# Turning three more q/k groups by GpSimd block copies, and issuing sixteen copies in two halves

## The chip, the core and the metric

The kernel runs on one core of one Trainium2 chip. Its time is the device time of one execution in microseconds (us), as the median of several runs. Five engines of the core matter: TensorE (PE in the profile; its weight loads are listed apart as PEld), VectorE (DVE), ScalarE (ACT), GpSimd (POOL) and SyncE (SP), which here only issues DMAs.

## What is computed

Two layers of a bidirectional encoder over 256 tokens of 2048 features, in float32. Each layer has a parallel mixer and a gated feed-forward part; the change lies in the mixer of the second layer. Cut to what matters here:

```python
for l in range(DEPTH):                                    # 2 layers
    h = rmsnorm(x, norm_mix[l]) * (1.0 + sc_a) + sh_a
    qa, ka, va, qb, kb, vb, ga, gb = split_cols(h @ w_in[l])
    qa = rotary_partial(rmsnorm(qa.reshape(B, S, HA, 128), qn_a[l]), pos)   # HA = 8 heads
    ka = rotary_partial(rmsnorm(ka.reshape(B, S, GA, 128), kn_a[l]), pos)   # GA = 2 heads
    ya = window_attention(qa, ka, va, sink_a[l]) @ w_proj_a[l]
    qb = rmsnorm(qb.reshape(B, S, HB, 128), qn_b[l])                        # HB = 8 heads
    kb = rmsnorm(kb.reshape(B, S, HB, 128), kn_b[l])
    yb = neighbourhood_attention(qb, kb, vb, rel_bias_b[l]) @ w_proj_b[l]
    merged = jax.nn.sigmoid(ga) * ya + jax.nn.sigmoid(gb) * yb
    x = x + gt_a * (merged @ w_out[l])
    ...
```

For the scores of a head, q and k are needed with the head's 128 features on the partitions. The projection gives them with tokens on the partitions, since the norm and the rotary tables work on rows. So each q/k block of 128 tokens by 128 features has to be transposed. The softmax probabilities p have to be transposed as well.

## The kernel before

**Weights and units.** All weights stream in as blocks of 128x128, sixteen to a *unit* of 1 MB. For each half unit ACT writes a rounded copy (L326, tile `hl`) and DVE writes the remainder (L327), so that TensorE can multiply in three passes: with the high part of the weight twice and with the low part once. The pool of `hl` has four buffers of half a unit. A unit is followed by a *tick* (`Stream.tick`), in which the background work of the pacer `bg` runs: functions that were deferred, then a share of the attention job.

**Groups.** The 4608 columns of q, k and v go in nine groups, numbered 0 to 8, of 512 columns and 64 blocks, that is four units and four ticks each (`tokens`, L406 to L408, 512 columns at a time). In the order of the code: 0 is k and v of the first mixer, 1 and 2 are its q; 3 is k, 4 is v and 5 is q of the first four heads of the second mixer; 6, 7 and 8 are the same of its last four. Before group 0 come eight units of a gate, after group 8 the rest of that gate.

**A q/k group** goes through `qk_rows`: ACT squares and sums (L578), DVE scales the sums (L471), GpSimd takes the inverse root (`qrs`, L472). Three ticks later DVE multiplies rows and roots into the tile `qn` (the norm, L588), of which there is one buffer. Another tick later `turn` transposes, in one of two ways:

- Not moved: eight transposes on TensorE (L624) into PSUM tiles `qtp`, which share the three buffers of the pool `ax` with the attention's scores, sums and outputs; ACT reads them out with the gain (L625).
- Moved (groups 0, 1, 2 and 8 of the second layer): DVE transposes within 32x32 blocks (L612), sixteen GpSimd copies put the blocks in place (`moved_blocks`, L298), and three ticks later (`QK_STEPS`) ACT scales them in place (L616), held in program order. The norm of a moved group is held in program order on DVE too.

**Attention.** In the second layer all sixteen heads transpose p the moved way: DVE (L304), sixteen GpSimd copies (`turned_blocks`), and one step of the attention job later ACT splits the result into `pT` (L418), held in program order. The job takes 0.4 steps a tick in the second layer, starts behind group 1, and takes in one new head a step.

**Order.** A planner orders each engine's instructions by their place in the program and by when it takes them to be ready; what is "held in program order" is not moved against its engine's other instructions. What a tick issues is thus a place in the order, and not a time.

Of the kernel before, what the change touches and what calls it, by code (L numbers as in the profile page):

```python
# [15 lines left out]
P = 128  # L16
# [5 lines left out]
HA, GA, HB = 8, 2, 8  # L22
# [8 lines left out]
BLOCK = 32  # L31
# [53 lines left out]
SCORES_3 = (1,)  # L85
EARLY = {1: 2}

MOVED_QK = [(), (0,1,2,8)]
QK_STEPS = 3
MOVED = [(0,0), (8,8)]  # L90
STEPS = [1, 1]
# [50 lines left out]
def encoder(ctx: ExitStack, tc: tile.TileContext, a: dict, out: bass.AP):  # L142
    nc = tc.nc
# [143 lines left out]
    def later(n, fn):  # L287

        if n == 0:
            fn()  # L290
        else:
            bg.defer(lambda: later(n - 1, fn))

    def moved_blocks(dst, src):

        for b in range(0, P, BLOCK):
            for a in range(0, P, BLOCK):
                nc.gpsimd.tensor_copy(  # L298
                    out=dst[a : a + BLOCK, :, :, b : b + BLOCK], in_=src[b : b + BLOCK, :, :, a : a + BLOCK]
                )  # L300

    def turned_blocks(src, rows, n):

        nc.vector.transpose(out=rows, in_=src)  # L304
        blocks = rows.rearrange("p t (n k) -> p n t k", n=n)
        dst = src.rearrange("p t (n k) -> p (t n k)", n=n).rearrange("p (n t k) -> p n t k", n=n, t=2)
        moved_blocks(dst, blocks)

    def unit_steps(l, u, by_halves=False):

# [256 lines left out]
            nc.vector.tensor_tensor(out=z[:], in0=ps[:, :S], in1=self.rbs[:], op=ALU.mult)  # L567
            return z, sh

    def qk_rows(pss, heads, rot, gain, dst, then, moved=False):  # L570

        cols = 0
        n = heads * HEAD
# [10 lines left out]
        def norm():  # L584
            qn = at.tile([P, 8 * HEAD], F32, name="qn", tag="qn", bufs=1)[:, : 2 * n]
            qn = qn.rearrange("p (t h d) -> p t h d", t=2, d=HEAD)
            for t, ps in enumerate(pss):
                product = nc.vector.tensor_tensor(  # L588
                    out=qn[:, t],
                    in0=ps[:, cols : cols + n].rearrange("p (h d) -> p h d", d=HEAD),  # L590
                    in1=rs[:, t * heads : (t + 1) * heads].unsqueeze(2).broadcast_to([P, heads, HEAD]),
                    op=ALU.mult,
                )
                if moved:
                    tc.keep_in_program_order(product)
            if rot is not None:
                x1, x2 = qn[:, :, :, :HALF], qn[:, :, :, HALF:ROT]
                tab = [rot[:, i].unsqueeze(2).broadcast_to([P, 2, heads, HALF]) for i in range(4)]
                tm = []
                for i in range(2):  # L600
                    z = ev.tile([P, S], F32, name=f"rt{i}", tag="z")
                    z = z[:].rearrange("p (i t h d) -> p i t h d", i=2, t=2, h=4)
                    tm += [z[:, 0, :, :heads], z[:, 1, :, :heads]]
                for i, src in enumerate((x1, x2, x2, x1)):
                    nc.vector.tensor_tensor(out=tm[i], in0=src, in1=tab[i], op=ALU.mult)
                nc.vector.tensor_tensor(out=x1, in0=tm[0], in1=tm[1], op=ALU.subtract)
                nc.vector.tensor_tensor(out=x2, in0=tm[2], in1=tm[3], op=ALU.add)
            bg.defer(lambda: turn(qn))

        def turn(qn):  # L610
            if moved:
                nc.vector.transpose(out=qn, in_=qn)  # L612
                moved_blocks(dst.rearrange("p h (t s) -> p h t s", t=2), qn.rearrange("p t h d -> p h t d"))

                def scaled():
                    tc.keep_in_program_order(nc.scalar.activation(out=dst, in_=dst, func=AF.Identity, scale=gain))  # L616
                    then()

                later(QK_STEPS, scaled)
                return  # L620
            for t in range(2):
                ps = ax.tile([P, 4, P], F32, name="qtp", tag="ax")
                for h in range(heads):
                    nc.tensor.transpose(ps[:, h], qn[:, t, h], ident[:])  # L624
                nc.scalar.activation(  # L625
                    out=dst[:, :, t * P : (t + 1) * P], in_=ps[:, :heads], func=AF.Identity, scale=gain
                )
            then()
# [17 lines left out]
    def attend(q, k, v, p, mask, scale, sink, o, rows=None):  # L646
# [161 lines left out]
    for l in range(L):  # L808
# [117 lines left out]
        for pi, (groups, gates) in enumerate(parts):  # L926
            last = pi == len(parts) - 1
            for g, part in enumerate(groups):
# [21 lines left out]
                    for t in range(2):  # L950
                        nc.scalar.copy(rows[:, t, vcol:], pss[t][:, vcol:])
                if g == 0:
                    qk_rows(pss, GA, rots[1], gains[:, 1:2], kTa, turned, g in MOVED_QK[l])
                elif g < 3:
                    qk_rows(pss, 4, rots[0], gains[:, 0:1], dst, turned, g in MOVED_QK[l])
# [248 lines left out]
```

## Time and profile before

| | us |
|---|---|
| median of 3 runs | 2656.88 |
| lowest and highest run | 2656.29, 2665.97 |
| profiled execution | 2655.52 |
| its span in the profile | 2653.7 |
| GpSimd busy in the whole span | 229.5 |
| of it copies of p (L298, 256 of them) | 147.5 |
| of it copies of q and k (L298, 64 of them) | 45.6 |

The profile is one execution. A row of the timeline has the start, the time taken, engine, line, operation, tile written and tiles read, shape and count, and in brackets the idle time of the engine before it and what ended that. A row of the waits has the waiting engine and line, what it waited for, the sum, how often and the longest. "Line" is the line of the kernel as printed above. TensorE's matmuls overlap: one is listed with its full duration, while the next starts before it ends, so what a matmul costs is read from starts.

### The profile page before, as it was taken

The page shows a single profiled execution, that of the slowest core. Times are in us where ns is not written, and L with a number is a line of the kernel's source. Part 1 is how long each engine was busy: PE and PEld are TensorE (multiplying, and loading weights), DVE is VectorE, ACT ScalarE, POOL GpSimd, SP SyncE. Part 2 cuts the span into 40 slices and gives each one's busy share as a digit, 9 for nine tenths or more (in the row PEclk, how much of TensorE's full clock was granted, in tenths as well). Part 3 has the DMA queues.
Part 4 walks back from the last instruction along what each step waited for, and adds up shares of the span by engine and source line. Part 5 has one row for each costly group of instructions (what it writes and reads, how often), then busy time and mean ns, then how long its engine had stood idle before and what let it go on. Part 6 is the DMA issues. An engine that isn't in the chain of part 4 may idle for free.

```text
span 2653.7 us, 51014 instructions
## 1 busy us (share of the span) xinstructions
PE 2640.4 (99%) x21164; PEld 2554.8 (96%) x21164; DVE 2122.8 (80%) x2979; ACT 1412.8 (53%) x2280; POOL 229.5 (9%) x345
## 2 busy tenths in 40 slices
PE   9999999999999999999999999999999999999999
PEld 7888899999999999999998889999999999999999
DVE  8898998997987888788976778868888866655664
ACT  5445865456653555355554666655565445544553
POOL 0001100000000000000002558620000000000000
PEclk9999999999999999999999999999999999999999
DMA  9987779885877778787856666667757765555554
GB/s 368 350 329 294 266 294 348 330 309 209 291 288 297 294 285 297 287 293 281 303 206 254 252 235 223 255 255 265 278 185 287 296 246 192 192 199 194 194 191 143
DMA packets 102042, 700.42 MB, mean 264 GB/s; under 512 B 12721, under 2 KB 15025, under 8 KB 17969
## 3 DMA queue, kind: packets, MB, share of 16 engines
q1 hardware_dynamic: 101810, 697.17, 71.5%
q8 instruction: 165, 2.70, 0.4%
q14 instruction: 67, 0.55, 0.1%
HBM read 695.03 MB, written 2.10 MB: 263 GB/s over the span
## 4 chain that ended last, share of the span: by engine, by line
PE 88%; DVE 6%; DMA 2%; issue 1%; ACT 1%; POOL 1%; SPq 0%; DVEq 0%; POOLq 0%; ACTq 0%
PE ps L343 25%; PE ps L345 25%; PE ps L344 25%; PE ps_t L407 4%; PE ps_t L408 4%; PE ps_t L406 4%; DVE hl L327 2%; DVE aw L233 2%; DMA aw<-in_aw 1%; PE sc L651 1%; PE po L689 1%; DMA w<-in_ws 1%; ACT hl L326 1%; POOL p L298 0%; POOL qrs L472 0%
## 5 line engine op out<-in xcount | busy, mean ns | idle before, releaser
L327 DVE TENSOR_TENSOR hl<-w,hl 128x1024 fp32r<-128x1024 f32 x928 | 1131.4, 1226 | 318.2 <-ACT hl L326 314.2
L326 ACT CAST hl<-w 128x1024 fp32r<-128x1024 f32 x928 | 970.3, 1049 | 744.0 <-PE ps L345 495.7
L343 PE MATMUL ps<-h,hl 128*128 128x256 f32 x3328 | 923.9, 278 | 1.3 <-DVE ya L970 0.6
L344 PE MATMUL ps<-h,hl 128*128 128x256 f32 x3328 | 921.1, 277 | 0.0
L345 PE MATMUL ps<-h,hl 128*128 128x256 f32 x3328 | 921.0, 277 | 0.0
L343 PEld LDWEIGHTS ps<-h,hl 128*128 128x128 f32 x3328 | 624.9, 188 | 2.3 <-DVE ya L970 0.8
L344 PEld LDWEIGHTS ps<-h,hl 128*128 128x128 f32 x3328 | 625.4, 188 | 0.4 <-DVE h L501 0.2
L345 PEld LDWEIGHTS ps<-h,hl 128*128 128x128 f32 x3328 | 624.4, 188 | 0.0
L233 DVE CUSTOM_DVE_ANT_0 aw<-aw,cact,ab 128x2048 f32<-128x2048 f32 x189 | 444.1, 2350 | 47.7 <-DMA aw<-in_aw 46.6
L407 PE MATMUL ps_t<-hl,h 128*128 128x512 f32 x576 | 225.3, 392 | 0.6
L406 PE MATMUL ps_t<-hl,h 128*128 128x512 f32 x576 | 223.3, 393 | 2.4 <-ACT h L500 1.6
L408 PE MATMUL ps_t<-hl,h 128*128 128x512 f32 x576 | 224.6, 391 | 0.0
L1049 DVE SCALAR_TENSOR_TENSOR u<-ps,cw,u 128x255 f32<-128x255 f32 x304 | 146.3, 481 | 71.9 <-ACT u L1047 67.9
L1047 ACT ACTIVATE u<-ps,cw 128x256 f32<-128x256 f32 x152 | 85.7, 564 | 192.3 <-PE ps L345 192.2
L345 PE MATMUL ps<-merged,hl 128*128 128x256 f32 x512 | 142.1, 278 | 0.5 <-DVE hl L327 0.4
L344 PE MATMUL ps<-merged,hl 128*128 128x256 f32 x512 | 141.7, 277 | 0.0
L343 PE MATMUL ps<-merged,hl 128*128 128x256 f32 x512 | 141.7, 277 | 0.0
L344 PE MATMUL ps<-act_o,hl 128*128 128x256 f32 x512 | 141.7, 277 | 0.0
L345 PE MATMUL ps<-act_o,hl 128*128 128x256 f32 x512 | 141.6, 277 | 0.0
L343 PE MATMUL ps<-act_o,hl 128*128 128x256 f32 x512 | 141.4, 277 | 0.0
L406 PEld LDWEIGHTS ps_t<-hl,h 128*128 128x128 f32 x576 | 108.0, 188 | 25.9 <-ACT h L500 2.7
L407 PEld LDWEIGHTS ps_t<-hl,h 128*128 128x128 f32 x576 | 108.2, 188 | 24.5 <-DVE hl L327 2.7
(244 smaller groups left out, 4805.6 us busy)
## 6 DMA issues: line engine op xcount, KB each, us to landing
w<-in_ws SPq DMA_DIRECT2D x463, 1024.0 KB, 4.9
aw<-in_aw SPq DMA_DIRECT2D x189, 1024.0 KB, 6.2
p<-in_bias SPq DMA_DIRECT2D x16, 256.0 KB, 4.4
x<-in_xT SPq DMA_DIRECT2D x4, 512.0 KB, 5.1
aw_o<-in_aw SPq DMA_DIRECT2D x2, 1024.0 KB, 12.6
out<-x SPq DMA_DIRECT2D x16, 128.0 KB, 3.3
w<-in_ws SPq DMA_DIRECT2D x2, 512.0 KB, 11.7
aw_b<-in_aw SPq DMA_DIRECT2D x1, 1024.0 KB, 18.3
```

Of the source, the lines that this page charges most:

```text
L233: nc.vector.tensor_tensor_reduce(out=raw[:], in0=raw[:], in1=cact[:], scale=1.0, scalar=ab[:, i : i + 1], op0=ALU.mult, op1=ALU.add, accum ...
L326: nc.scalar.copy(hl[:, 0], r)
L327: nc.vector.tensor_tensor(out=hl[:, 1], in0=r, in1=hl[:, 0].bitcast(F32), op=ALU.subtract)
L343: nc.tensor.matmul(out, hi, act[0], start=first, stop=False)
L344: nc.tensor.matmul(ps[:, :S], hi, act[1], start=False, stop=False)
L345: nc.tensor.matmul(out, lo, act[0], start=False, stop=last)
L406: nc.tensor.matmul(ps[:], xh, hi, start=kc == kcs[0], stop=False)
L407: nc.tensor.matmul(ps[:], xh, lo, start=False, stop=False)
L408: nc.tensor.matmul(ps[:], xl, hi, start=False, stop=kc == kcs[-1])
L651: nc.tensor.matmul(sc[:, t], q[i][:, t * P : (t + 1) * P], k[j], start=i + j == 0, stop=(i, j) == by(q)[-1])
L1047: nc.scalar.activation(out=u, in_=ps, func=AF.Identity, scale=w[:, 1:2], bias=w[:, 3:4])
L1049: nc.vector.scalar_tensor_tensor(out=u[:, to], in0=ps[:, of], scalar=w[:, j : j + 1], in1=u[:, to], op0=ALU.mult, op1=ALU.add)
```

## The change

Three things change:

- Groups 3, 5 and 6 of the second layer are moved too, so that all its q/k groups are. Their gain (L616) is issued five ticks behind the turn instead of three (`gain_late`).
- `moved_blocks` issues eight of its sixteen copies at once and defers the other eight by one tick. For a head's p the second eight are issued at the latest ahead of the split into `pT` (`rest()`). This holds for all moved groups and for all sixteen heads of the second layer.
- Which norms are held in program order is now a parameter of its own (`pinned`), true for all groups of the second layer. They are also all the moved ones, so groups 3, 5 and 6 gain the hold.

```diff
-MOVED_QK = [(), (0,1,2,8)]
+MOVED_QK = [(), (0,1,2,3,5,6,8)]
...
+    def once(fn):
+
+        due = [fn]
+
+        def run():
+            if due:
+                due.pop()()
+
+        return run
+
     def moved_blocks(dst, src):
 
-        for b in range(0, P, BLOCK):
-            for a in range(0, P, BLOCK):
-                nc.gpsimd.tensor_copy(
-                    out=dst[a : a + BLOCK, :, :, b : b + BLOCK], in_=src[b : b + BLOCK, :, :, a : a + BLOCK]
-                )
+        def half(first):
+            for b in range(first, first + P // 2, BLOCK):
+                for a in range(0, P, BLOCK):
+                    nc.gpsimd.tensor_copy(
+                        out=dst[a : a + BLOCK, :, :, b : b + BLOCK], in_=src[b : b + BLOCK, :, :, a : a + BLOCK]
+                    )
+
+        half(0)
+        rest = once(lambda: half(P // 2))
+        later(1, rest)
+        return rest
...
-        moved_blocks(dst, blocks)
+        return moved_blocks(dst, blocks)
...
-    def qk_rows(pss, heads, rot, gain, dst, then, moved=False):
+    def qk_rows(pss, heads, rot, gain, dst, then, moved=False, pinned=False, gain_late=False):
...
-                if moved:
+                if pinned:
                     tc.keep_in_program_order(product)
...
-                later(QK_STEPS, scaled)
+                later(QK_STEPS + (2 if gain_late else 0), scaled)
...
-            turned_blocks(p[:], rows(), 2)
+            rest = turned_blocks(p[:], rows(), 2)
             for _ in range(STEPS[sink is None]):
                 yield
+            rest()
...
-                    qk_rows(pss, 4, None, gains[:, 3:4] if g in (3, 6) else gains[:, 2:3], dst, turned, g in MOVED_QK[l])
+                    qk_rows(pss, 4, None, gains[:, 3:4] if g in (3, 6) else gains[:, 2:3], dst, turned, g in MOVED_QK[l], l == 1, g in (3, 5, 6))
```

The two other calls of `qk_rows`, for groups 0 to 2, get the same two arguments.

More of the change, by code (lines that the diff above doesn't have):

```diff
@@ L952, in encoder @@
                 if g == 0:
-                    qk_rows(pss, GA, rots[1], gains[:, 1:2], kTa, turned, g in MOVED_QK[l])
+                    qk_rows(pss, GA, rots[1], gains[:, 1:2], kTa, turned, g in MOVED_QK[l], l == 1, g in (3, 5, 6))
                 elif g < 3:
-                    qk_rows(pss, 4, rots[0], gains[:, 0:1], dst, turned, g in MOVED_QK[l])
+                    qk_rows(pss, 4, rots[0], gains[:, 0:1], dst, turned, g in MOVED_QK[l], l == 1, g in (3, 5, 6))
                 elif vcol is None:
-                    qk_rows(pss, 4, None, gains[:, 3:4] if g in (3, 6) else gains[:, 2:3], dst, turned, g in MOVED_QK[l])
+                    qk_rows(pss, 4, None, gains[:, 3:4] if g in (3, 6) else gains[:, 2:3], dst, turned, g in MOVED_QK[l], l == 1, g in (3, 5, 6))
                 else:
```

## The prediction

> **What bounds the kernel now.** I read the page first (busy shares and the chain of waits).
>
> ```profile
> PE 2640.4 (99%) x21164; PEld 2554.8 (96%) x21164; DVE 2122.8 (80%) x2979; ACT 1412.8 (53%) x2280; POOL 229.5 (9%) x345
> ```
>
> ```profile
> POOL 0001100000000000000002558620000000000000
> ```
>
> ```profile
> PE 88%; DVE 6%; DMA 2%; issue 1%; ACT 1%; POOL 1%; SPq 0%; DVEq 0%; POOLq 0%; ACTq 0%
> ```
>
> TensorE is busy for 99% of the span and carries 88% of the chain: work taken from it is time, as long as the others keep feeding it. GpSimd is nearly idle as a whole, but the second part, in 40 slices, shows where it works: one slice of 66 us at 80%. That is the stretch that the change loads further, so averages say nothing here and I looked at the stretch alone, by windows (columns: stretch, length, busy time of PE, PEld, DVE, ACT and POOL, clock, DMA).
>
> ```profile
> 1486.00:1595.00 109.00, 107.79 (x517) 90.03 (x516) 80.93 (x133) 70.74 (x147) 53.60 (x103) 1.00 0.62 231
> 1595.00:1618.00 23.00, 23.00 (x164) 21.48 (x163) 18.14 (x27) 15.33 (x40) 17.33 (x26) 1.00 0.58 212
> ```
>
> These 132 us hold groups 4 to 8 of the second layer, the turning of groups 3, 5 and 6, and the first attention heads. TensorE idles for 109.00 - 107.79 = 1.2 us in all of them. DVE has 132 - 99 = 33 us free, ACT 46, GpSimd 61; the clock is 1.00. So there are two things to ask: what the removed TensorE work is worth, and whether the added DVE and GpSimd work makes something late that TensorE waits for.
>
> **What is removed.** First the transposes of groups 3, 5 and 6 (tile view of the transposes' result, 1400 to 1700 us), then how the first eight stand in TensorE's timeline, then the second eight and what followed them.
>
> ```profile
> L624 PE MATMUL qtp<-ident,qn x24: 270/273/273, 1504.9 to 1580.5; 128*128 128x128 f32 x24
> L625 ACT ACTIVATE packB<-qtp,gains x6: 669/690/694, 1505.6 to 1581.3; 128x512 f32<-128x512 f32 x6
> ```
>
> ```profile
> 1504.71 0.39 PE L408 MATMUL ps_t<-hl,h 128*128 128x512 f32 x1
> 1504.94 1.03 PE L624 MATMUL qtp<-ident,qn 128*128 128x128 f32 x8
> 1505.73 0.48 PE L406 MATMUL ps_t<-hl,h 128*128 128x512 f32 x1
> 1506.05 0.39 PE L407 MATMUL ps_t<-hl,h 128*128 128x512 f32 x1
> ```
>
> ```profile
> 1552.38 1.03 PE L624 MATMUL qtp<-ident,qn 128*128 128x128 f32 x8
> 1553.16 0.95 PE L689 MATMUL po<-pT,vA 128*128 128x256 f32 x6
> 1553.95 0.39 PE L406 MATMUL ps_t<-hl,h 128*128 128x512 f32 x1
> 1555.41 0.95 PE L651 MATMUL sc<-kA,qA 128*128 128x256 f32 x6 [1.06 <-ACT packB L625]
> ```
>
> Matmuls overlap, so a duration is not what one costs; starts are. The transposes start 0.23 us behind the matmul before them (1504.71, 1504.94), as one such matmul does behind another. Without the eight, L406 would start at 1504.94 and L407 at 1505.17; it starts at 1506.05. Eight transposes cost 0.88 us, and three times that is **-2.6 us**.
>
> The last fence shows a second cost. After L406 at 1553.95 the scores should start at 1554.18 and start at 1555.41, 1.2 us late, put down to ACT's L625: the scores need a PSUM buffer of the three that they share with the transposes' results, and ACT must first read those out. Without transposes there is nothing to read out: **-1.2 us**, the whole idle time of that window. A bound on the other side is 0, if the scores then wait for some other buffer; I take the row.
>
> ACT loses six L625 and gains three L616 of twice the size.
>
> ```profile
> L616 ACT ACTIVATE packB<-packB,gains x1: 1154/1154/1154, 1636.8 to 1636.8; 128x1024 f32<-128x1024 f32 x1
> ```
>
> ```profile
> L612 DVE STREAM_TRANSPOSE qn<-qn x4: 706/1239/1246, 1430.8 to 1617.1; 128x1024 f32<-128x1024 f32 x3, 128x512 f32<-128x512 f32 x1
> ```
>
> That is 6 x 0.69 - 3 x 1.15 = 0.7 us less, under its 46 us of free time: 0. DVE gains three L612 of 1.24 us, 3.7 us against 33 free: 0 by themselves, 3.7 if each fell where TensorE waits for DVE.
>
> **What is added on GpSimd.** 48 copies of 32x256. The GpSimd timeline around them:
>
> ```profile
> 1451.96 14.58 POOL L298 COPY packA<-qn 32x256 f32<-32x256 f32 x16 [5.72 <-DVE qn L612]
> ...
> 1501.54 9.90 POOL L298 COPY p<-spare 32x128 f32<-32x128 f32 x16 [12.49 <-DVE spare L304]
> ...
> 1532.29 6.30 POOL L298 COPY p<-packA 32x128 f32<-32x128 f32 x16 [7.02 <-DVE packA L304]
> 1538.67 1.63 POOL L472 TENSOR_TENSOR qrs<-qss,mhalf 128x8 f32<-128x8 f32 x1
> 1553.04 7.64 POOL L298 COPY p<-packA 32x128 f32<-32x128 f32 x16 [12.73 <-DVE packA L304]
> 1560.76 1.63 POOL L472 TENSOR_TENSOR qrs<-qss,mhalf 128x8 f32<-128x8 f32 x1
> 1569.27 10.38 POOL L298 COPY p<-packA 32x128 f32<-32x128 f32 x16 [6.87 <-DVE packA L304]
> 1583.15 9.75 POOL L298 COPY p<-packA 32x128 f32<-32x128 f32 x16 [3.51 <-DVE packA L304]
> 1595.02 11.84 POOL L298 COPY p<-packA 32x128 f32<-32x128 f32 x16 [2.11 <-DVE packA L304]
> 1609.18 1.64 POOL L472 TENSOR_TENSOR qrs<-qss,mhalf 128x8 f32<-128x8 f32 x1 [2.32 <-DVE qss L471]
> 1613.15 10.62 POOL L298 COPY p<-packA 32x128 f32<-32x128 f32 x16 [2.33 <-DVE packA L304]
> 1623.83 11.64 POOL L298 COPY packB<-qn 32x256 f32<-32x256 f32 x16
> ```
>
> Sixteen such copies took 14.58 us (group 1) and 11.64 us (group 8). Three times that is 35 to 44 us, against 61 free: it fits as a sum, at 82 to 88% of the engine. So the question is order. Three engines wait for these copies: ACT (L418 casts p, L616 scales; both are held in program order, so its weight casts L326 stand behind), and DVE (the norm L588 cannot overwrite qn before the copies have read it, and it waits for qrs, which queues behind copies; its weight subtractions L327 stand behind).
>
> Group 3: GpSimd's work before head 0, the qrs of this group, ends at 1501.54 - 12.49 = 1489.05. A norm (1.29 for its two halves, in a row below) and a transpose later it is some 1492; GpSimd is idle until 1501.54. Its copies fill 1492 to 1504 or 1507, and head 0's end 2 to 5 us later than now. Group 5: behind the qrs that ends at 1538.67 + 1.63 = 1540.3 come norm, weight work and transpose, so its copies fall between some 1545 and 1560, in the 12.73 us in which GpSimd idles now, and partly into head 3's. Group 6: its norm ends at 1562.43 + 1.29 = 1563.7 (row below), so they are ready from about 1565, ahead of head 4's, which move by 11.6 to 14.6 us and push heads 5 and 6.
>
> The eight-and-eight matters here. At 1532.29 the sixteen copies of a head run ahead of a qrs, and the norm waited for it. The waits of 1486 to 1618 and the second such case:
>
> ```profile
> DVE qn L588 <- POOL qrs L472: 11.6, 3, 5.7
> ...
> PEld ps_t L407 <- DVE hl L327: 0.6, 1, 0.6
> ```
>
> ```profile
> 1559.32 0.17 DVE L471 TENSOR_SCALAR qss<-qss 128x8 f32<-128x8 f32 x1 [0.44 <-ACT qsq L578]
> ...
> 1562.43 1.29 DVE L588 TENSOR_TENSOR qn<-ps_t,qrs 128x512 f32<-128x512 f32 x2 [2.94 <-POOL qrs L472]
> ```
>
> This calibrates what lateness costs: DVE stood still for 11.6 us in three waits, and TensorE waited once for DVE's L327, 0.6 us in its weight loader, because weights are split some 5 us ahead (four half-unit buffers of 2.7 us each, two of them in use). The point where that lead was used up is the one behind the norm at 1562.43; there, every further microsecond is a microsecond of TensorE. With halves the qrs can go ahead of the last eight copies: up to 1.3 us earlier (its sums were ready at 1559.32 + 0.17 = 1559.5, and it began at 1560.76), and that wait goes: -0.6. Or head 3's first eight, behind group 5's sixteen, push it: 1545 + 14.6 + 3.8 = 1563.4 instead of 1560.76, +2.7. Between -0.6 and +2.7 I take +0.8, nearer the gain, as GpSimd is idle for 12.73 us before head 3. That is the one new cost on the path.
>
> ACT's held casts of p, by ACT's timeline, for the two heads most exposed:
>
> ```profile
> 1512.78 0.62 ACT L418 CAST pT<-p 128x512 fp32r<-128x512 f32 x1
> ...
> 1587.50 0.62 ACT L418 CAST pT<-p 128x512 fp32r<-128x512 f32 x1
> ```
>
> Head 0's copies end at 1511.44 now, 1.3 us before its cast; 2 to 5 later makes ACT wait 0.7 to 3.7. Head 4's end at 1579.65, 7.9 us before; 11.6 to 14.6 later makes ACT wait 3.7 to 6.7. ACT has 46 of 132 us free and casts weights some 5 us ahead of their use: I take 0, with up to 3.7 + 6.7 = 10.4 us if none of it is hidden.
>
> Splitting the heads' own copies (16 heads) moves eight copies back in the order by one weight unit, 24 matmuls x 0.23 = 5.5 us of TensorE. It adds no copy; where GpSimd is backlogged it changes nothing. 0.
>
> **Sum:** -2.6 - 1.2 + 0.8 = -3.0 us. The profiled execution took 2655.52 (span 2653.7 and 1.8 around it), so 2652.5; it lies 1.4 below the median of the runs, and from that it is 2653.9. I forecast 2653.7.
>
> **The rivals.** *Slower: GpSimd's queue runs late (20%).* The place is 1569 to 1624: 10.38 + 9.75 + 11.84 + 1.64 + 10.62 = 44 us of work in 54.5; group 6 makes it 56 to 59, so the queue overflows into group 8's copies, and the casts held for heads 0 and 4 wait up to 10.4 us. For it: the overflow is arithmetic. Against: the 11.6 us of DVE waits that cost 0.6. It decides once a held wait exceeds the lead of some 5 us. Two thirds of 10.4 unhidden is +7, less 3: +4, 2661. If the casts of heads 5, 6 and 7 came as late as head 4's, 3 x 6.7 = 20 us more, it would pass +13.
>
> *Nothing comes of it (13%).* The saved 3.8 us return as waits for weight halves, through the 3.7 us of L612: 2656.9. Against: of the stretch's 1.2 us of idle TensorE the read-out of the transposes has 1.06, L327 next to nothing.
>
> *Copies and DVE block each other (5%).* These rows stand for it and against it:
>
> ```profile
> L298 POOL COPY packA<-qn x48: 279/395/2365, 1431.7 to 1486.9; 32x256 f32<-32x256 f32 x32, 32x128 f32<-32x128 f32 x16
> ```
>
> ```profile
> L327 DVE TENSOR_TENSOR hl<-w,hl x38: 1180/1224/1310, 1490.3 to 1599.7; 128x1024 fp32r<-128x1024 f32 x38
> ```
>
> A copy takes 0.395 us at the median and up to 2.365: it waits for something as long as a DVE instruction. DVE's subtraction hardly stretches (1.224, at most 1.310). If each of 16 copies of group 5 held DVE for a whole 0.4 us just where the lead is used up, that is 6.4 us, less 3: +3.4, 2660. The Trainium skill (SBUF — State Buffer, section "SBUF: two separate sides") says that GpSimd and a DVE operation with two SBUF inputs take one shared port pair as an exclusive lock for a whole instruction, and the other blocks. By that rule both sides pay; the trace agrees for the copies' side, and shows 0.09 us at most on DVE's durations.
>
> **How the numbers follow.** The forecast has 62%; its own range is 2651.3 to 2656.6 (-0.6 and +2.7 in place of +0.8, and a microsecond for the spread of the runs). The range is 2650.5 to 2661.0: down to everything gained, counted from the profiled execution (2655.5 - 2.6 - 1.2 - 0.6 = 2651.1, and a little), up to the queue's rival. 0.5% of this kernel is 13 us, about what a measurement can tell from no change. All of TensorE's work and idle time at stake is 4.4 us, so faster by 13 is 2%, for a gain I don't see. Slower by 13 is the queue's rival at its worst: 8%. The rest, 90%, is no difference.
>
> **What would show it.** Right: no L624 in the second layer; TensorE's idle time in 1486 to 1595 under 1.5 us; the end of group 8 some 3 us earlier, counted from the start of group 3; GpSimd at 80% or more there; the qrs at 1538 and 1560 no later than now. Wrong: TensorE waiting for DVE's L327 or ACT's L326 by several us; ACT's L418 or L616 listed as waiting for GpSimd's L298 for over 5 us; DVE's L588 waiting for copies; DVE's L327 stretched.

## The result, and the profile after

| | before | after |
|---|---|---|
| median of 15 runs each, us | 2656.55 | 2667.56 |
| lowest and highest | 2654.03, 2667.57 | 2663.27, 2671.49 |
| profiled execution | 2655.52 | 2667.3 |
| its span | 2653.7 | 2665.5 |

The ratio of the times is 1.0028 with a 95% interval of 1.0019 to 1.0037: slower by some 7.4 us (5.0 to 9.8). The medians differ by more, 11.0 us; four of the fifteen runs of before took 2663 to 2668. As a time the result lies outside the forecast's range; as a change it lies within the 0.5% that were called no difference.

The first part of the page of after, and its chain:

```profile
PE 2644.7 (99%) x21140; PEld 2557.4 (96%) x21140; DVE 2126.6 (80%) x2982; ACT 1406.9 (53%) x2277; POOL 274.3 (10%) x393
...
PE 85%; DVE 7%; POOL 4%; issue 2%; ACT 2%; DMA 1%; SPq 0%; DVEq 0%; POOLq 0%; ACTq 0%
```

The 24 transposes are gone (21164 matmuls became 21140), yet TensorE is busy for longer. GpSimd took 44.8 us more and went from 1% to 4% of the chain. To place the loss, two distances serve for every kernel below. The *stretch* is from the first to the last start of the groups' first weight pass (L406 before, L422 after). The *path* runs from that first start to the first matmul that reads oB, the second mixer's projection; it also holds what follows group 8. The rows of before, by source line, and those of after:

```profile
L406 PE MATMUL ps_t<-hl,h x288: 387/390/476, 1395.1 to 1603.2; 128*128 128x512 f32 x144
L343 PE MATMUL ps<-oB,hl x128: 275/277/283, 1793.4 to 1836.9; 128*128 128x256 f32 x128
```

```profile
L422 PE MATMUL ps_t<-hl,h x288: 387/389/632, 1398.3 to 1614.0; 128*128 128x512 f32 x144
L359 PE MATMUL ps<-oB,hl x128: 275/276/283, 1805.2 to 1848.7; 128*128 128x256 f32 x128
```

The stretch grew from 208.1 to 215.7 us (+7.6), the path from 398.3 to 406.9 (+8.6). The remaining 3.2 us between the two profiled executions lie ahead of group 0, where the change touches nothing; the interval of the ratio holds 8.6. So 7.6 of the 8.6 us are lost by the last start of group 8. Both distances are read from one profiled execution of each kernel. Kernels that run the same instructions in the same order (after and e1, before and e18 below) agree in them within 0.4 us, while group 0 starts anywhere from 1393.5 to 1400.1 us in the kernels' profiles; so the distances are the finer measure. The windows of after (columns as before):

```profile
1486.00:1595.00 109.00, 102.66 (x472) 84.88 (x472) 79.55 (x122) 66.10 (x144) 84.95 (x128) 0.98 0.58 209
1595.00:1618.00 23.00, 20.79 (x96) 17.23 (x95) 13.06 (x20) 12.93 (x28) 20.55 (x41) 0.93 0.58 224
1581.50:1585.00 3.50, 3.50 (x10) 2.76 (x11) 3.50 (x5) 0.00 (x0) 3.33 (x5) 0.57 0.46 108
1612.50:1615.50 3.00, 3.00 (x10) 2.38 (x9) 1.34 (x2) 0.73 (x4) 2.75 (x7) 0.54 0.99 341
```

TensorE idles for 6.3 + 2.2 = 8.5 us where it idled for 1.2, and in two short windows the granted clock is 0.57 and 0.54. GpSimd works for 84.95 + 20.55 = 105.5 of the 132 us, that is 80%, just under the forecast's 82 to 88%. Yet the sum is not what matters; its timeline is:

```profile
1501.85 13.74 POOL L309 COPY packB<-qn 32x256 f32<-32x256 f32 x16 [8.57 <-DVE den L682]
1515.64 6.46 POOL L309 COPY p<-spare 32x128 f32<-32x128 f32 x16
1526.81 12.21 POOL L309 COPY p<-packA 32x128 f32<-32x128 f32 x16 [4.72 <-DVE packA L320]
1539.82 7.12 POOL L309 COPY p<-packA 32x128 f32<-32x128 f32 x16 [0.81 <-DVE packA L320]
1547.02 1.64 POOL L488 TENSOR_TENSOR qrs<-qss,mhalf 128x8 f32<-128x8 f32 x1
1551.32 16.16 POOL L309 COPY packB<-qn 32x256 f32<-32x256 f32 x16 [2.66 <-DVE qn L628]
1567.52 9.00 POOL L309 COPY p<-packA 32x128 f32<-32x128 f32 x16
1576.60 1.64 POOL L488 TENSOR_TENSOR qrs<-qss,mhalf 128x8 f32<-128x8 f32 x1
1580.31 10.29 POOL L309 COPY p<-packA 32x128 f32<-32x128 f32 x16 [2.07 <-DVE packA L320]
1590.66 13.60 POOL L309 COPY packB<-qn 32x256 f32<-32x256 f32 x16
1604.32 5.21 POOL L309 COPY p<-packA 32x128 f32<-32x128 f32 x16
```

Times of before and after are compared from the start of group 0, so 3.2 us are taken off those of after. Group 3's copies start at 1501.85 (1498.7 in the time of before, not 1492), after 8.57 us in which GpSimd idled, and head 0's come behind them. (They wait for the transpose L628, which ends at 1501.7 in DVE's rows below; the row names a short DVE instruction behind it.) From there to 1609.5 GpSimd stands for only 10.3 of 107.7 us. The halves never part (sixteen in a row each time), and group 5's root stands behind sixteen copies of a head: it ends at 1548.7, 1545.5 in the time of before, that is 5.2 us later than before (1540.3). Group 5's copies run where head 3's stood. What waits for this, from the waits of 1486 to 1618:

```profile
DVE qn L604 <- POOL qrs L488: 10.4, 2, 5.9
...
PE ps_t L423 <- DVE hl L343: 8.5, 4, 3.0
...
DVE packA L320 <- POOL p L309: 8.3, 2, 7.1
ACT pT L434 <- POOL p L309: 6.9, 1, 6.9
```

and how one such wait arises and gets to TensorE, in DVE's timeline and in TensorE's:

```profile
1493.53 1.28 DVE L604 TENSOR_TENSOR qn<-ps_t,qrs 128x512 f32<-128x512 f32 x2
...
1500.48 1.24 DVE L628 STREAM_TRANSPOSE qn<-qn 128x1024 f32<-128x1024 f32 x1
...
1524.90 1.23 DVE L343 TENSOR_TENSOR hl<-w,hl 128x1024 fp32r<-128x1024 f32 x1 [0.58 <-ACT hl L342]
...
1541.61 1.23 DVE L343 TENSOR_TENSOR hl<-w,hl 128x1024 fp32r<-128x1024 f32 x1 [0.57 <-ACT hl L342]
1548.69 1.29 DVE L604 TENSOR_TENSOR qn<-ps_t,qrs 128x512 f32<-128x512 f32 x2 [5.85 <-POOL qrs L488]
1550.01 1.25 DVE L628 STREAM_TRANSPOSE qn<-qn 128x1024 f32<-128x1024 f32 x1
1551.18 2.52 DVE L343 TENSOR_TENSOR hl<-w,hl 128x1024 fp32r<-128x1024 f32 x2
```

```profile
1526.21 0.47 PE L423 MATMUL ps_t<-hl,h 128*128 128x512 f32 x1
...
1552.42 0.50 PE L423 MATMUL ps_t<-hl,h 128*128 128x512 f32 x1 [2.67 <-DVE hl L343]
...
1581.34 0.50 PE L423 MATMUL ps_t<-hl,h 128*128 128x512 f32 x1 [2.97 <-DVE hl L343]
...
1582.23 0.63 PE L423 MATMUL ps_t<-hl,h 128*128 128x512 f32 x1
1582.65 0.63 PE L424 MATMUL ps_t<-hl,h 128*128 128x512 f32 x1
1583.08 0.63 PE L422 MATMUL ps_t<-hl,h 128*128 128x512 f32 x1
```

Group 3's transpose comes 7 us behind its norm, with weight work and head 0's softmax in between. Later DVE writes the remainder of a half unit at 1541.61, stands for 5.85 us before the norm that is held in its place, then norms and transposes; the next remainder comes 9.6 us behind the last, and TensorE stands for 2.67 us.

In before the same norm waited for almost as long (5.66 us, until 1540.34) and TensorE did not stand. The difference is the lead, the time from the end of a remainder on DVE to the first matmul that uses it (L407 before, L423 after). Ahead of that wait in before it was 7.2 us (the remainder of 1533.27 ended at 1534.50 and was used at 1541.69). In after it was 5.45 us for the last remainder ahead of head 0's wait on ACT (6.91 us, shown further below) and 0.1 us for the next one, which ended at 1526.13 and was used at 1526.21. When group 5's norm began to wait it was back at 4.0 us (1542.84 to 1546.86).

The account for the path: 8.5 us of stalls, and 2 x 3.41 x 0.5 = 3.4 us for the lower clock (in the trace it is 0.50 from 1582.01 to 1585.43 and from 1612.73 to 1616.15; the two short windows lie across these edges), less what the removed work saves (4.3, measured below), give +7.6; the path grew by 8.6. The last 1.0 us is not accounted for.

### The profile page after: what moved, and what is told of

Its sections match the earlier page's. It is cut to its first block, busy times and chain, and to the rows that moved or that the text cites. A ratio compares the mean times of both kernels' runs of the same rounds, so it can differ in the third digit from the quotient of the medians.

```text
span 2665.5 us, 51013 instructions
## 1 busy us (share of the span) xinstructions
PE 2644.7 (99%) x21140; PEld 2557.4 (96%) x21140; DVE 2126.6 (80%) x2982; ACT 1406.9 (53%) x2277; POOL 274.3 (10%) x393
## 4 chain that ended last, share of the span: by engine, by line
PE 85%; DVE 7%; POOL 4%; issue 2%; ACT 2%; DMA 1%; SPq 0%; DVEq 0%; POOLq 0%; ACTq 0%
PE ps L359 25%; PE ps L361 25%; PE ps L360 25%; PE ps_t L424 3%; PE ps_t L423 3%; PE ps_t L422 3%; DVE hl L343 2%; POOL p L309 2%; DVE aw L233 2%; POOL packB L309 2%; DMA aw<-in_aw 1%; ACT hl L342 1%; PE po L706 1%; PE sc L667 1%; POOL qrs L488 0%
## 5 line engine op out<-in xcount | busy, mean ns | idle before, releaser
L342 ACT CAST hl<-w 128x1024 fp32r<-128x1024 f32 x928 | 969.1, 1049 | 698.6 <-PE ps L361 490.6
L423 PE MATMUL ps_t<-hl,h 128*128 128x512 f32 x576 | 226.7, 394 | 8.9 <-DVE hl L343 8.5
L422 PE MATMUL ps_t<-hl,h 128*128 128x512 f32 x576 | 224.0, 394 | 2.2 <-ACT h L516 1.6
L423 PEld LDWEIGHTS ps_t<-hl,h 128*128 128x128 f32 x576 | 108.7, 189 | 34.5 <-DVE hl L343 12.1
L422 PEld LDWEIGHTS ps_t<-hl,h 128*128 128x128 f32 x576 | 108.5, 189 | 26.1 <-ACT h L516 2.7
```

What stands on the lines that cost most here:

```text
L342: nc.scalar.copy(hl[:, 0], r)
L422: nc.tensor.matmul(ps[:], xh, hi, start=kc == kcs[0], stop=False)
L423: nc.tensor.matmul(ps[:], xh, lo, start=False, stop=False)
```

## The experiments

The question is which of these made it late: the split, one of the groups, the copies' own length on GpSimd, the contention with DVE, the norm's place, or a buffer that neighbours share. All kernels start from after. The table gives each one's change of stretch and path against before, and its ratio to runs of before that were made along with it; medians of different rows were not taken together, so they compare through the ratios.

| run | stretch | path | median, us | ratio, 95% interval |
|---|---|---|---|---|
| after | +7.6 | +8.6 | 2667.56 | 1.0028, 1.0019 to 1.0037 |
| e1_no_split | +8.0 | +8.4 | 2663.96 | 1.0025, 1.0014 to 1.0036 |
| e3_only3 | +4.1 | +4.2 | 2659.29 | 1.0013, 1.0003 to 1.0022 |
| e4_only5 | +3.1 | +3.2 | 2659.28 | 1.0013, 1.0003 to 1.0022 |
| e5_only6 | -1.3 | -1.3 | 2655.80 | 0.9996, 0.9987 to 1.0005 |
| e6_not_pinned | +6.7 | +7.5 | 2662.74 | 1.0023, 1.0013 to 1.0032 |
| e7_one_copy | -4.4 | -4.3 | 2651.15 | 0.9981, 0.9971 to 0.9990 |
| e8_dve_copies | +5.3 | +5.4 | 2658.93 | 1.0012, 1.0003 to 1.0022 |
| e9_act_copies | +7.1 | +7.2 | 2662.36 | 1.0023, 1.0013 to 1.0032 |
| e10_own_rows | +3.7 | +4.7 | 2660.97 | 1.0019, 1.0009 to 1.0028 |
| e11_held_copies | +6.2 | +9.0 | 2666.70 | 1.0037, 1.0024 to 1.0050 |
| e13_held_rows | +1.1 | +3.9 | 2661.08 | 1.0015, 1.0006 to 1.0025 |
| e14_only6_rows | -1.3 | -1.2 | 2654.53 | 0.9993, 0.9984 to 1.0003 |
| e15_56_rows | -1.2 | +4.1 | 2659.36 | 1.0008, 0.9999 to 1.0017 |
| e16_56_held_rows | -2.7 | +2.6 | 2656.48 | 1.0002, 0.9993 to 1.0011 |
| e17_56_late | -3.2 | -3.1 | 2653.77 | 0.9988, 0.9979 to 0.9997 |
| e18_before_rows | +0.2 | +0.3 | 2655.50 | 0.9998, 0.9990 to 1.0007 |
| e19_356_late | +1.7 | +3.1 | 2658.96 | 1.0008, 0.9999 to 1.0017 |

### The split: e1_no_split

```diff
         half(0)
-        rest = once(lambda: half(P // 2))
-        later(1, rest)
-        return rest
+        half(P // 2)
+        return lambda: None
```

> The changed kernel without the split: sixteen copies are issued at once again. In the profile of the changed kernel the two halves of every sixteen run back to back, with no other GpSimd work between them, so the split moved nothing: stretch 215 to 216.5, time within 2 us of the changed kernel's 2667.6. If the split by itself delays heads (second half a unit later), it is faster by 3 us or more.

The path is +8.4 against +8.6 with the split; the intervals of the ratios overlap. The instructions stand in the same order on TensorE, DVE, ACT and GpSimd as in after. The median is 3.6 us below that of after, more than the 2 us that were expected; in the profiled executions, 4.3 us apart, 4.1 us of this lie ahead of group 0. So the split does nothing: issuing eight copies a tick later only gave them a later place in the program, and the planner puts them back behind the first eight.

### One group at a time: e3_only3, e4_only5, e5_only6

```diff
-MOVED_QK = [(), (0,1,2,3,5,6,8)]
+MOVED_QK = [(), (0,1,2,3,8)]      # e3; 5 in place of 3 in e4, 6 in e5
...
-... g in MOVED_QK[l], l == 1, g in (3, 5, 6))
+... g in MOVED_QK[l], g in MOVED_QK[l], g in (3, 5, 6))
```

> Of groups 3, 5 and 6 only group 3 goes by copies; 5 and 6 by TensorE as before. Queue theory: the chain of GpSimd that ended late began with group 3's sixteen copies, which push head 0 and by it the later heads; a part of the stalls stays: stretch 208 to 212, time 2657 to 2661. Hold theory: group 3's norm stops DVE once, where weights are well ahead: stretch 207, time 2655.5.

> Of groups 3, 5 and 6 only group 5 goes by copies. It takes away the scores' wait of 1.2 us as well as 0.9 us of transposes. Queue theory: GpSimd has no backlog before it, but its copies stand ahead of head 3's and of the root of group 6, whose norm has no lead: stretch 206 to 210, time 2655 to 2659, so that the three alone (with group 3's +4 and group 6's -1.3 of stretch) add up to less than the +7.6 of all, as a backlog does not build up. If the costs are each group's own, they add up: group 5 alone has then some +5, stretch 213, time 2661.

> Of groups 3, 5 and 6 only group 6 goes by copies. Queue theory: by then GpSimd has no backlog; group 6's copies push heads 5 and 6, whose casts have 8 to 12 us to spare: stretch 206.5 to 208.5, time 2655 to 2657.5. Hold theory: group 6's norm is the one at which weights run out of lead, so this is the worst of the three: stretch 209 to 212, time 2658 to 2662.

Group 3 alone costs 4.2 us, group 5 alone 3.2, group 6 alone gains 1.3, about a third of the 4.3 that all three can give. Together that is +6.1 of the +8.6; the rest is put down to their meeting. In e3 and e4 TensorE has one stall of over 2 us each (3.09 and 3.90 us), followed by one stretch of 3.41 us at half the clock; in e5 it has neither. So the place that the forecast feared least (groups 3 and 5, in GpSimd's idle time) costs, and the one that it feared most (group 6, the queue of 1569 to 1624) does not when it is moved alone. The stretch of e3 (212.2) lies at the upper end of what was expected; e4's (211.2) lies between its two expectations (206 to 210 and 213); e5's stretch and time lie within theirs.

### The length of the copies: e7_one_copy, e8_dve_copies, e9_act_copies

```diff
+        if few:                                    # e7, groups 3, 5 and 6
+            nc.gpsimd.tensor_copy(out=dst, in_=src)
+            return lambda: None
...
-                    nc.gpsimd.tensor_copy(
+                    (nc.vector if few else nc.gpsimd).tensor_copy(          # e8
+                    (nc.scalar.copy if few else nc.gpsimd.tensor_copy)(     # e9
```

> The changed kernel, but for groups 3, 5 and 6 one GpSimd copy of 128x1024 stands in place of the sixteen 32x256 (the blocks then lie in the wrong places: the blocks' exchange is left out for these groups). Holds, gains and transposes stay. Queue theory (GpSimd's serial chain makes heads and norms late): the groups' stretch, from the first to the last row matmul of groups 0 to 8, 208.1 us before and 215.7 after, falls to 204 to 206, and the time to 2653 to 2655. Hold theory (norms and gains held in program order stop DVE and ACT whatever GpSimd does): the stretch stays at 213 to 216 and the time at 2664 to 2668.

> The changed kernel, with the 48 copies of groups 3, 5 and 6 on DVE in place of GpSimd. Estimate: 256 elements a row on DVE, by the subtraction's 1.22 us for 1024, are 0.3 us, so 48 are 15 us of DVE's 33 free in the stretch. Queue theory: GpSimd has its load of before, stretch 204 to 207, time 2653 to 2656. If DVE, and not GpSimd, is what TensorE waited for (its 3.7 us of transposes and its order), it gets worse: stretch over 214, time over 2665.

> The changed kernel, with the 48 copies of groups 3, 5 and 6 on ACT in place of GpSimd. Estimate: by the cast of 128x256 at 0.40 us, 48 are 19 us of ACT's 46 free in the stretch. Queue theory: stretch 204 to 207, time 2653 to 2656, if ACT's lead holds where sixteen copies stand in a row (6.4 us against some 5 us of lead): then up to 2 us more for each group, 2659 at most.

e7 leaves out the exchange of the blocks for groups 3, 5 and 6, so its output is not that of the kernel. The same transposes, norms, holds and gains stand, and GpSimd has one copy a group; its copies of qn and its matmuls by source line:

```profile
L307 POOL COPY packB<-qn x3: 1042/1042/1947, 1502.0 to 1583.0; 128x1024 f32<-128x1024 f32 x3
...
L426 PE MATMUL ps_t<-hl,h x288: 389/389/398, 1398.4 to 1602.1; 128*128 128x512 f32 x144
L363 PE MATMUL ps<-oB,hl x128: 276/276/283, 1792.4 to 1835.8; 128*128 128x256 f32 x128
```

Three copies of 1 to 2 us in place of 41.6 us of copies: the path is 394.0, 4.3 less than before and 12.9 less than after (the stretch of 203.7 and the time lie 0.3 and 1.9 us below what was expected of the queue theory). All that was lost is lost through the sixteen copies a group on GpSimd: of the 12.9, 8.5 us are TensorE's stalls and 3.4 its time at half the clock, neither of which e7 has. What the removed TensorE work is worth is measured too: the forecast had 2.6 + 1.2 = 3.8 for it, 4.4 with the 0.6 of the norm's wait.

Moved to DVE or ACT, the copies are shorter but don't pay either, by source line:

```profile
L309 DVE COPY packB<-qn x48: 270/286/373, 1499.2 to 1589.5; 32x256 f32<-32x256 f32 x48
```

```profile
L309 ACT COPY packB<-qn x48: 400/403/408, 1498.8 to 1589.7; 32x256 f32<-32x256 f32 x48
```

48 x 0.286 = 13.7 us on DVE, which had 33 free, cost 9.7 us against e7; 19.3 on ACT, which had 46 free, cost 11.5. Both expectations, built on free time, fell. The waits of 1486 to 1618 say where most of it went; first e8, then e9:

```profile
PE ps_t L423 <- DVE hl L343: 5.7, 3, 2.2
```

```profile
PE ps_t L423 <- DVE hl L343: 3.7, 5, 1.1
...
PE ps_t L422 <- ACT hl L342: 2.7, 1, 2.7
```

Besides, each has 6.8 us at half the clock in its trace, 3.4 us lost. That makes 5.7 + 3.4 = 9.1 of the 9.7 us, and 3.7 + 2.7 + 3.4 = 9.8 of the 11.5. By its length a block of 16 x 0.286 = 4.6 us (DVE) or 6.4 us (ACT) ahead of a weight half is about as long as the lead of some 5 us; that this is the whole cause was not tried.

### The norm's place: e6_not_pinned

```diff
-... g in MOVED_QK[l], l == 1, g in (3, 5, 6))
+... g in MOVED_QK[l], l == 1 and g in (0, 1, 2, 8), g in (3, 5, 6))
```

> The changed kernel, with the norms of groups 3, 5 and 6 not held in program order on DVE. Hold theory: stretch back to 204 to 206, time 2653 to 2655. Queue theory: the number of copies is the same, but group 3's transpose stands some 6 us earlier in DVE's order, so its copies use GpSimd's idle time ahead of head 0: the stretch falls by a part only, to 209 to 213, time 2658 to 2664, and GpSimd is still over 80% busy from 1500 to 1600.

GpSimd's timeline of e6:

```profile
1491.25 15.52 POOL L309 COPY packB<-qn 32x256 f32<-32x256 f32 x16 [3.74 <-DVE qn L628]
1506.81 9.28 POOL L309 COPY p<-spare 32x128 f32<-32x128 f32 x16
```

This profile's group 0 starts at 1393.5, 4.8 us earlier than in after, so group 3's copies start at 1496.1 in the time of after instead of 1501.85. DVE takes the transpose right behind a norm that isn't held, with one weight remainder between. So the hold moved these copies back by 5.8 us. Yet only 1.1 us of the path come back; the time lies in the range expected of the queue theory, the stretch (214.8) 1.8 us above its upper end. The norm's place is real, and not the main loss.

### The shared rows: e10_own_rows

DVE transposes p of head i into rows that lie in the places of q of heads i-1 and i; the next head's rows overlap by one place, so DVE must wait until GpSimd has read them. The edit gives neighbouring heads places that don't overlap (heads 0 and 2 use a spare tile):

```diff
-                return qTa[:, i - 1 : i + 1] if i else paired(F32, f"spare{l}")
+                if not spares:
+                    spares.append(paired(F32, f"spare{l}"))
+                at = (None, 0, None, 2, 0, 4, 2, 6)[i]
+                return spares[0] if at is None else qTa[:, at : at + 2]
```

> The changed kernel, with other homes for the transposed rows of the first mixer's heads: neighbouring heads no longer share one (heads 0 and 2 use the spare tile, 1 and 4 q's places 0 and 1, 3 and 6 places 2 and 3, 5 places 4 and 5, 7 places 6 and 7). The order of every engine is the same, only DVE's transpose of a head need not wait until GpSimd has read the rows of the head before. If that wait hands the lateness on (8.3 us of DVE waiting for GpSimd's copies in the changed kernel), the stretch falls from 215.7 to 209 to 213 and the time to 2659 to 2664. If GpSimd's load alone sets it, DVE only runs further ahead and the stretch stays at 214.5 to 216, the time at 2665 to 2668.

The order on the four engines is that of after, and the path is 3.9 us shorter; stretch and time lie in the range expected. So the waits in the row "DVE packA L320 <- POOL p L309" of after (8.3 us, the longest 7.1), off everything that the forecast had looked at, carried nearly half of the +8.6. In e18_before_rows the groups are those of before, with these rows and the split:

```diff
-MOVED_QK = [(), (0,1,2,3,5,6,8)]
+MOVED_QK = [(), (0,1,2,8)]
```

> The kernel before (no further group moved), with separate homes for the rows of neighbouring heads: the control for the rows. Before, no DVE wait on those rows is listed, so nothing changes: stretch 208.1, time within 1 us of before.

It is as fast as before (path +0.3): the shared rows cost nothing as long as GpSimd is on time. They pass lateness on; they don't make it.

### Halves that do interleave: e11_held_copies, e13_held_rows

e11 holds all copies and the roots of the second layer in program order on GpSimd; e13 has that and the rows of e10.

```diff
-                    nc.gpsimd.tensor_copy(...)
+                    tc.keep_in_program_order(nc.gpsimd.tensor_copy(...))
...
-        nc.gpsimd.tensor_tensor(out=dst, in0=src, in1=mhalf[:, :k], op=ALU.pow)
+        root = nc.gpsimd.tensor_tensor(out=dst, in0=src, in1=mhalf[:, :k], op=ALU.pow)
+        if st.l:
+            tc.keep_in_program_order(root)
```

> The changed kernel, with GpSimd's copies and the second layer's roots held in program order, so that the second eight copies really stand a tick behind and the roots of groups 5, 6 and 8 go ahead of eight or sixteen copies. If the roots behind the copies hand the lateness to DVE (10.4 us of waits in the changed kernel), the stretch falls from 215.7 to 207 to 212, time 2655 to 2662. If the whole load of GpSimd sets it, whatever its order, the stretch stays at 214 or more; the halves of groups 0 and 1, which now stand behind the next group's root, can only make it later.

> Both: copies and roots held in program order, and separate homes for the rows of neighbouring heads. If both waits of DVE on GpSimd hand the lateness on, each by its own share (rows alone gave -3.9 of stretch), the stretch is 204 to 208 and the time 2652 to 2657, with all three groups moved. If ACT's held casts of p are what is left, 208 to 211, 2657 to 2660.

e11's GpSimd timeline shows the order that the change describes:

```profile
1553.66 9.86 POOL L309 COPY packB<-qn 32x256 f32<-32x256 f32 x8
1563.56 3.71 POOL L309 COPY p<-packA 32x128 f32<-32x128 f32 x8
1567.35 3.69 POOL L488 TENSOR_TENSOR qrs<-qss,mhalf 128x8 f32<-128x8 f32 x1
```

By itself it doesn't help the path (+9.0; the stretch of 214.3 is that of the second expectation, 214 or more): GpSimd has the same work, and DVE waits 9.1 us for the shared rows where it waited 8.3. With rows of their own it does: e13 has a stretch of only +1.1, against +3.7 for the rows alone, in the range expected if ACT's held casts are what is left (208 to 211; the time is 1 us above its 2660). By e13's waits:

```profile
ACT pT L434 <- POOL p L309: 15.0, 2, 10.5
```

Head 0's cast, held in ACT's order, waits for 10.5 us behind group 3's copies, until 1522.71; TensorE's longest stall in e13's groups, 2.36 us, ends at 1525.49 with a weight cast of ACT (L342). And 2.8 us are lost only after the groups (path +3.9, stretch +1.1).

### Without group 3, and later gains: e14, e15, e16, e17, e19

e14 is e5 with the rows of e10. e15 moves groups 5 and 6 with these rows (group 3's norm is not held then); e16 also holds copies and roots. e17 is e16 with the gains of groups 0 and 8 two ticks later too; e19 is e17 with group 3 as well.

```diff
-MOVED_QK = [(), (0,1,2,3,5,6,8)]
+MOVED_QK = [(), (0,1,2,5,6,8)]           # e15, e16, e17
...
-... g in MOVED_QK[l], g in (3, 5, 6))
+... g in MOVED_QK[l], g in (0, 3, 5, 6, 8))   # e17, e19
```

> Of groups 3, 5 and 6 only group 6 goes by copies, and neighbouring heads have separate rows: the mildest change that takes TensorE work away. Group 6 alone had a stretch of 206.8 and 5.0 us of DVE waiting for a head's rows. Without that wait: 206.5 to 207, time 2654.5 to 2656, that is 0 to -2 against before.

> Groups 5 and 6 by copies, group 3 by TensorE, separate rows, nothing held on GpSimd. If what is left is group 5's and head 3's copies ahead of group 6's root (the 4 us stall of group 5 alone), it stays: stretch 208 to 211. If that stall came from the backlog of group 3, it is gone: 205.5 to 207, time 2653 to 2655.

> The same with GpSimd's copies and roots held in program order, so that group 6's root stands between the halves. If the root behind 32 copies was group 5's stall, it goes: stretch 205 to 207, time 2652 to 2655. Compared with all three groups held (209.2) the difference is group 3's: its copies ahead of head 0's, for which ACT's cast waited 10.5 us. If group 3 is not what is left there, this stays at 208 to 209.

> Groups 5 and 6 by copies, separate rows, GpSimd held in program order, and the gains of groups 0 and 8 two ticks later too. In the run without the last edit the groups' stretch was 205.4 (2.7 less than before), and all was lost again in one stall of 2.4 us at 1662, behind ACT's held gain of group 8, which waited 6.7 us for its copies. If that held gain is the stall, it goes and the gain of 2.8 us stays: time 2652.5 to 2654.5. If not, 2656 as without the edit.

> The same with all three groups: against its like without the later gains (stretch 209.2, time 2661) the stall at 1662 goes: 2656 to 2659. What is left against e17 is group 3's: 2 to 4 us, by its copies ahead of head 0's.

e14 equals e5, although DVE waits 5.0 us for a head's rows in e5: where the lead is whole, a wait of that length costs nothing. In e15 and e16 the stretch is shorter than before (-1.2, -2.7) as expected, but the path is longer, and the times miss the 2653 to 2655 and 2652 to 2655 expected: 5.3 us are lost in both behind group 8. e16's ACT timeline and its waits of 1640 to 1670 show where:

```profile
1644.67 1.16 ACT L634 ACTIVATE packB<-packB,gains 128x1024 f32<-128x1024 f32 x1 [6.74 <-POOL packB L309]
```

```profile
PE ps L361 <- DVE hl L343: 2.5, 2, 2.3
```

Group 8's gain, three ticks behind the turn and held on ACT, meets copies that GpSimd has not done; ACT stands for 6.74 us, and TensorE for 2.3, followed by 3.41 us at half the clock. Two ticks more for that gain, and for group 0's, is the edit of e17:

```profile
L422 PE MATMUL ps_t<-hl,h x288: 387/389/477, 1394.3 to 1599.2; 128*128 128x512 f32 x144
L359 PE MATMUL ps<-oB,hl x128: 276/276/283, 1789.5 to 1832.9; 128*128 128x256 f32 x128
```

The path is 395.2, 3.1 less than before, and the ratio 0.9988 (0.9979 to 0.9997): faster than before and after, if by little (the interval just leaves out 1), and in the range expected. That is about 2/3 of the 4.3 us, and two of the three groups are moved. TensorE has no stall and no time at half the clock in the path. e19 puts group 3 back with all these remedies; its time is as expected, but it costs 6.2 us of path against e17, more than the 2 to 4 expected for group 3; its ACT again waits 10.6 us for head 0's copies. Which of the edits that make e17 is needed on top of the later gains, and which of the two later gains, was not tried one by one.

## Why the prediction failed, by its own steps

The step that failed is the one on what GpSimd's added copies cost. The sum had +0.8 us for it, "the one new cost on the path"; after less e7 is 12.9. Term by term:

**Removed work: right.** 2.6 + 1.2 forecast, 4.3 measured by e7 with the 0.6 of the norm's wait. L612 and L616 cost nothing there, as said, so the rival by which nothing comes of the change is out too.

**GpSimd's time: the sum right, the places wrong.** The forecast took 35 to 44 us of copies (41.6 measured; with the 71 us that GpSimd worked before they make 80 to 87% of 132, not 82 to 88) and fitted them into gaps: 1492 to 1507 for group 3, 1545 to 1560 for group 5. Group 3's copies came 6.7 us later (1498.7 in the time of before), because the transpose stood 7 us behind the norm, the norm being held. The forecast let the transpose follow at once ("and a transpose later it is some 1492") and did not look at what DVE had to do there. Head 0's copies end at 1515.64 + 6.46 = 1522.1, 1518.9 in the time of before, beside 1511.4: 7.5 us late, and not the "2 to 5" of the forecast. Head 2's copies and group 5's root then reached 5.2 us into the gap before head 3, group 5's copies ran to 1564.3 in the time of before instead of 1560, and head 3's to 1573.3, 12.6 us later than before.

**ACT's held casts at 0: wrong.** The cast of head 0 in ACT's timeline of after:

```profile
1522.13 0.62 ACT L434 CAST pT<-p 128x512 fp32r<-128x512 f32 x1 [6.91 <-POOL p L309]
```

The wait for head 0 is 6.91 us, above the 0.7 to 3.7 of the forecast and above the lead of some 5 us. It stops nothing by itself, but it takes the lead from 5.45 to 0.1 us, and the stalls follow. Head 4's cast, which the forecast had as the longest (3.7 to 6.7), is not in the list. Its 11.6 to 14.6 us of delay left out that the copies ready from 1565 would first fill GpSimd's idle time up to 1569.27; with that it is 7.3 to 10.3, and the wait at most 2.4. In after group 6's copies (1590.66) even stand behind head 4's (1580.31). That a held wait decides once it exceeds the lead was the rival's rule; the forecast applied it to the wrong head.

**The norm of group 6 at +0.8: mis-sized.** In place of one wait with -0.6 to +2.7 there were two norms that waited for 10.4 us, group 5's for 5.85 and group 6's for 4.54, and the stalls behind them. In sum the norms waited for less than before (11.6 us in three). The rivals' "11.6 us of DVE waits that cost 0.6" was read as if the lead hid waits in general. In before the waits met leads of 5.9, 7.2 and 8.4 us. In after the norms' waits meet a lead that earlier waits have used (4.0 us ahead of group 5's norm, 0.3 ahead of group 6's), and the wait of 7.1 us for the shared rows meets one of 4.6: four stalls, 8.5 us.

**Splitting at 0: right**, for a simpler reason than said: the order doesn't change at all (e1). That the root could go ahead of the last eight copies was wrong: in after both roots shown follow sixteen.

**What was missing: the shared rows and the clock.** The rows of neighbouring heads overlap, so a late head makes the next head's transpose late on DVE: 7.1 us in one wait, 3.9 us of path (e10). And behind two of the four stalls the granted clock was 0.50 for 3.41 us each, with starts 0.42 apart (1582.23, 1582.65, 1583.08) instead of 0.23: 3.4 us that no engine's busy time shows. The Trainium skill (TensorE: Matmul & The Clock Gate, section "Part 1: The HAM clock gate (the "warmup" mystery)") has the half rate as what follows an idle window of about 3.4 us; the trace agrees on the rate, yet here stalls of 2.97 and 2.21 us were enough, and one of 2.67 was not. In after's trace the two half-rate stretches begin 30.72 us apart, nine times their length of 3.41. Counted in steps of that length, the two stalls put 2.75 and 2.14 us of idle time into the step just ahead of the half rate; the stall of 2.67 us lies across an edge, as 1.54 and 1.13.

**The rivals.** The queue's rival had the right kind (a held wait beyond the lead; +4 forecast, +8.6 on the path), at the wrong place: 1569 to 1624 by group 6, which alone gains 1.3 us (e5). The rival of the blocked port: DVE's subtraction hardly stretched again, by groups of lines and shapes from 1490 to 1615:

```profile
L343 DVE TENSOR_TENSOR hl<-w,hl 128x1024 fp32r<-128x1024 f32 x38 | 47.5, 1265 | 7.4 <-ACT hl L342 7.2
...
L309 POOL COPY packB<-qn 32x256 f32<-32x256 f32 x48 | 41.6, 867 | 13.2 <-DVE den L682 8.6 <-DVE qn L628 2.7
```

1.265 us at the mean, where it was 1.237 in before from 1490 to 1615: 38 x 0.03 = 1.1 us of DVE. GpSimd pays, with 0.867 us a copy. In after's trace from 1400 to 1750 us, the 22 copies of 32x256 that ran while DVE stood took 0.390 to 0.398 us each; the 48 that met a subtraction of DVE took 1.30 us at the median, about the length of that subtraction. So this rival was right about the copies, and it is part of why they are long; that DVE is held up in turn, which its +3.4 us rested on, did not show.

## What to carry to other kernels

An engine that is free for a share of a stretch can still be late in it: write down when each added job can start, with what stands ahead of it on the engine that feeds it, and what is queued behind, before fitting it into a gap. A lead of 5 us hides one wait of 5 us and not a row of them; look for the waits that hand lateness on, above all for instructions held in program order and for buffers that neighbours share, which cost nothing until something is late. Issuing something later is only another priority where a planner sets the order; if the order matters it has to be held, and then every held wait has to have room, as the gain of group 8 did in the kernel that was faster.

## What the runs showed of the hardware

The copies of group 8 in before, by source line:

```profile
L298 POOL COPY packB<-qn x16: 391/396/1458, 1623.8 to 1635.1; 32x256 f32<-32x256 f32 x16
```

A block copy of 32x256 that took 0.39 us at its quickest took 0.87 at the mean beside DVE's weight work in after (1.30 at the median of those that met a subtraction), while a subtraction of DVE took some 0.03 us longer than before: nearly the whole price of the meeting falls on GpSimd. One copy of 128x1024 there took 1.04 us at the median (e7), less than a tenth of the 13.6 to 16.2 us that sixteen block copies of the same number of elements took in after. And two of the three TensorE stalls of over 2 us in after were followed by 3.41 us at half the clock, 1.7 us lost each, so such a stall can cost half as much again. In the traces of all nineteen kernels, start and end of the execution aside, 17 of 21 stalls of over 2 us were followed by such a stretch, and none came without such a stall.
